# Seven-product projections: order of the combined activation blocks, banks of two kinds for transposes, and weight block sums emitted one step earlier

## The chip, the cores and the metric

The kernel runs on one core of a Trainium2 chip. A core has a matmul engine (TensorE, "PE" in the profile), a vector engine (VectorE, "DVE"), a scalar engine (ScalarE, "ACT"), GpSimd ("POOL") and SyncE ("SP", which here mostly starts DMAs). Each of them runs its own instructions strictly in the order written, and they meet at semaphores. The metric is the device time of one execution in microseconds; the number that counts is the median over runs of the same kernel.

## The reference

Two layers over a sequence of 1024 tokens of width 1024, all in fp32. Layer 0 has a gated delta network as its mixer, layer 1 a retention mixer; each is followed by a residual layer norm and a convolutional feed-forward block with hidden width 2816:

```python
for i in range(DEPTH):
    mod = (e @ ada_w[i] + ada_b[i])[:, None, :]
    sh1, sc1, g1, sh2, sc2, g2 = jnp.split(mod, 6, axis=-1)
    y = mixers[i % N_MIXERS](x * (1.0 + sc1) + sh1)
    x = layer_norm(DN_ALPHA * x + (1.0 + g1) * y, ln_g[i, 0], ln_b[i, 0])
    y = conv_ffn(x * (1.0 + sc2) + sh2, ffn_up[i], ffn_conv_w[i], ffn_conv_b[i], ffn_down[i])
    x = layer_norm(DN_ALPHA * x + (1.0 + g2) * y, ln_g[i, 1], ln_b[i, 1])

def conv_ffn(h, w_up, conv_w, conv_b, w_down):
    gate, up = jnp.split(h @ w_up, 2, axis=-1)
    gate = causal_dwconv(gate, conv_w) + conv_b
    return (jax.nn.silu(gate) * up) @ w_down
```

What the change touches are the large products of this: `h @ w_up` of both feed-forward blocks, the query, key and gate projections of the retention, and the three products that come back to width 1024 (`@ w_down` twice, the retention's `@ w_out` once).

## The kernel before, in words

**Precision.** Every fp32 operand of a product is split into a high part (ACT copies it to the fp32r type) and a low part (DVE subtracts the high part): the helper `split`, lines 89 and 90. A product is then three matmuls, low by high, high by low and high by high: lines 110 to 112 in the helper `mm3`. Line 90 on DVE is therefore the last step before PE can use any operand, and rows such as `wb L90` or `T L90` are named by the tile that was split.

**Seven products instead of eight.** A product of two 2 by 2 block matrices is done with seven block products (the Winograd form of Strassen's scheme). Two generators do this. `strassen` serves the projections whose activations stay in SBUF. Its activations are the blocks 11, 21, 12, 22 and four combinations: T1 = 12 - 11, T2 = 22 - T1, T3 = T2 - 11 (which is 22 - 12) and T4 = 21 - T2. Each block is four tiles, k = 0 to 3. `build_T` makes them, once for each of three projections (feed-forward 0 up at about 790 us, retention at about 1480 us, feed-forward 1 up at about 2345 us). I call these three places the borders. At a border the first two weight pairs (items 0 and 1) are multiplied plainly: `side(n, 0)` uses the blocks 11 and 21, `side(n, 1)` the blocks 12 and 22. `side(0, 0)` and `side(1, 0)` run while the rest of the activations are still being normalised; then `build_T` transposes the tiles of the lower half (four PE transposes into one PSUM bank, line 406; ACT scales and shifts the bank into a tile `bt`, line 408) and splits the blocks 12 and 22; then come `side(0, 1)`, the function `rest`, which makes T1 to T4, and `side(1, 1)`. From item 2 on, `wino` runs the seven products in the order 11, 21, T1, T2, 22, T3, T4. Its weights are combined by DVE into a PSUM bank (`psub`, line 1203: s1, s2, s4, s3) and split into a tile `wb`. The block 11 exists only as a high and a low part, so that adding it needs the sum of the two again: `joined` makes it with two matmuls by the identity into a PSUM bank (line 414).

**The way back.** `proj_gen` serves the three products that return to width 1024. The activation blocks, combined beforehand, are read from DRAM (tile `ar`, split to `ab`). The weight blocks are combined on the fly by `bblk` on DVE, for the products T1 (line 1302), T2 (line 1305, in place) and T4 (line 1308); the sum is split to `bb`. Each product has 11 steps (8 in the retention), and one step's work is emitted by `ops`. The weight blocks are loaded three steps ahead by `load_b`. When a product ends, its `f` function takes the four accumulators on DVE; `f2`, after the second product, makes the four tiles `c` (line 1383).

**Banks.** PSUM has eight banks of 128 by 512 floats: four with the tag `acc`, two with `mm`, two with `sc`. The transposes of `build_one` (line 259, for the blocks 11 and 21 while `proj_ln` or `proj_gen` still runs), those of `build_T` (line 406), `joined` and `psub` all draw from the two `mm` banks. The two `sc` banks serve every third product of `wino`, half of the accumulators in two of the products of `proj_gen`, and the squares of the layer norm.

**What sets the order.** The text of the kernel gives the dependencies. A scheduler then orders each engine's instructions once, by its own estimates of times, and the engines follow that order. So a change in the text shows only as far as it changes these orders.

## Time and profile before

| what | value |
|---|---|
| time, median of 3 runs | 3016.57 us (3015.99 to 3017.25) |
| profiled execution, its own time | 3017.08 us |
| its span, first to last instruction | 3015.3 us |
| granted TensorE clock, mean over the span | 0.975 |
| busy: PE, DVE, ACT, POOL | 94%, 73%, 45%, 21% |

A row of the timeline shows the start, the duration, the engine, the line of the kernel, the operation and its tiles; in brackets stands how long the engine was idle before it and what ended that idle time. A row of the groups shows the busy time, the mean duration, and after the bar the idle time ahead of the group. A row of the windows shows a stretch, its length, the busy time (and number of instructions) of PE, of its weight loads (PEld), of DVE, ACT and POOL, then the granted clock, the DMA share and the GB/s.

### The profile page before, as it was taken

Reading aid. Unit: us, or ns where it says so; the run is one execution under the profiler, and the core shown is the slowest. Engines: PE = TensorE matmul, PEld = TensorE weight load, DVE = VectorE, ACT = ScalarE, POOL = GpSimd, SP = SyncE. Lnnn points to the kernel's source line nnn. Section 1 sums busy time; section 2 is a strip of 40 time slices with the busy share of each in tenths; the row PEclk is TensorE's granted clock in tenths of the full one; section 3 lists DMA queues with packets and bytes.
Section 4 is the critical chain, followed back from the end, with each engine's and each line's share of the span. In section 5 each row is a group of like instructions: output and inputs, shape, how many; then the busy total and the mean of one; then the engine's idle time right before and its main releaser. Section 6 shows DMA issues by size and latency. Waiting matters only on the chain.

```text
span 3015.3 us, 38927 instructions
## 1 busy us (share of the span) xinstructions
PE 2843.1 (94%) x13638; PEld 2313.8 (77%) x13638; DVE 2196.9 (73%) x3845; ACT 1349.4 (45%) x2513; POOL 637.6 (21%) x629
## 2 busy tenths in 40 slices
PE   8889998999989999999999999989999899999997
PEld 7768877887768878777777787767777688888785
DVE  5795687545578888997688745556688787778888
ACT  4655555434544444536533343222336544445444
POOL 0411221133011111520023302522201011113503
PEclk9999999999999999999999999999999999999998
DMA  7222221343344444863423444656563333335652
GB/s 271 84 74 71 95 92 64 115 158 136 109 140 159 156 153 148 308 205 126 154 84 112 171 157 136 209 168 189 190 234 118 115 133 105 105 105 211 229 174 106
DMA packets 238708, 442.36 MB, mean 147 GB/s; under 512 B 22448, under 2 KB 75952, under 8 KB 238512
## 3 DMA queue, kind: packets, MB, share of 16 engines
q1 hardware_dynamic: 207328, 392.16, 38.6%
q10 hardware_dynamic: 29760, 43.00, 3.9%
q0 software_dynamic: 1424, 4.72, 0.4%
q8 instruction: 107, 1.75, 0.2%
q14 instruction: 89, 0.73, 0.1%
HBM read 331.26 MB, written 108.53 MB: 146 GB/s over the span
## 4 chain that ended last, share of the span: by engine, by line
PE 58%; DVE 16%; DMA 10%; issue 8%; ACT 4%; POOL 2%; SPq 1%; POOLq 0%; DVEq 0%; ACTq 0%
PE acc L635 14%; PE acc L1418 8%; PE acc L1157 6%; PE acc L110 4%; PE acc L111 4%; PE acc L112 4%; PE sc L1157 3%; PE sc L635 3%; PE mm L635 2%; PE sc L1418 2%; DVE ab L90 1%; PE sc L111 1%; PE sc L110 1%; PE sc L112 1%; DVE wb L90 1%
## 5 line engine op out<-in xcount | busy, mean ns | idle before, releaser
L1418 PE MATMUL acc<-bb,ab 128*128 128x512 f32 x1800 | 432.5, 393 | 7.7 <-DVE bb L90 5.8
L1418 PEld LDWEIGHTS acc<-bb,ab 128*128 128x128 f32 x1800 | 337.0, 189 | 85.0 <-DVE bb L90 10.3
L635 PE MATMUL acc<-hT,wh 128*128 128x512 f32 x960 | 302.6, 397 | 0.0
L1556 POOL TENSOR_TENSOR o<-o 128x512 f32<-128x512 f32 x88 | 119.0, 1363 | 723.8 <-DVE o L1549 716.1
L1157 PE MATMUL acc<-T,wb 128*128 128x512 f32 x840 | 209.6, 400 | 15.1 <-DVE wb L90 15.1
L635 PEld LDWEIGHTS acc<-hT,wh 128*128 128x128 f32 x960 | 184.2, 192 | 34.6
L635 PE MATMUL acc<-hT,wl 128*128 128x512 f32 x480 | 204.4, 426 | 0.2 <-ACT sg L1083 0.2
L1157 PEld LDWEIGHTS acc<-T,wb 128*128 128x128 f32 x840 | 160.6, 192 | 54.0 <-DVE wb L90 20.3
L90 DVE TENSOR_TENSOR ab<-ar,ab 128x512 fp32r<-128x512 f32 x210 | 179.4, 862 | 29.4 <-ACT ab L89 29.3
L89 ACT ACTIVATE ab<-ar 128x512 fp32r<-128x512 f32 x210 | 128.4, 623 | 134.3 <-PE acc L1418 73.3
L90 DVE TENSOR_TENSOR wb<-wr,wb 128x512 fp32r<-128x512 f32 x162 | 114.8, 711 | 100.1 <-ACT wb L89 97.3
L90 DVE TENSOR_TENSOR wl<-wr,wh 128x1024 fp32r<-128x1024 f32 x85 | 107.4, 1264 | 89.2 <-ACT wh L89 89.2
L89 ACT ACTIVATE wh<-wr 128x1024 fp32r<-128x1024 f32 x101 | 106.8, 1058 | 122.0 <-PE acc L635 55.7
L1214 ACT ACTIVATE pc<-acc 128x512 f32<-128x512 f32 x143 | 84.8, 593 | 169.5 <-PE acc L1157 98.6
L90 DVE TENSOR_TENSOR wb<-mm,wb 128x512 fp32r<-128x512 f32 x216 | 145.0, 684 | 21.2 <-ACT wb L89 19.2
L89 ACT ACTIVATE wb<-mm 128x512 fp32r<-128x512 f32 x216 | 122.5, 594 | 66.4 <-DVE mm L1203 66.3
L89 ACT ACTIVATE wb<-wr 128x512 fp32r<-128x512 f32 x162 | 98.8, 626 | 97.6 <-DMA wr<-in_ffn_up 51.3
L635 PE MATMUL acc<-wh,hT 128*128 128x512 f32 x384 | 137.1, 420 | 2.0 <-DVE vv L90 2.0
L1535 DVE SCALAR_TENSOR_TENSOR o<-g,vc,o 128x512 f32<-128x512 f32 (+2 forms) x176 | 135.8, 790 | 1.3 <-ACT o L1530 0.7
L454 DVE SCALAR_TENSOR_TENSOR qkv<-raw,vc,qkv 128x512 f32<-128x512 f32 x144 | 114.6, 800 | 25.9 <-ACT qkv L452 24.8
L89 ACT ACTIVATE bb<-Br 128x512 fp32r<-128x512 f32 x120 | 74.0, 624 | 123.1 <-DVE Br L1302 61.8
L110 PE MATMUL acc<-T,wb 128*128 128x512 f32 x292 | 116.3, 398 | 9.9 <-DVE wb L90 9.4
(618 smaller groups left out, 7148.3 us busy)
## 6 DMA issues: line engine op xcount, KB each, us to landing
wr<-in_ffn_up SPq DMA_DIRECT2D x96, 512.0 KB, 4.2
mvw<-in_ada_w SPq DMA_DIRECT2D x80, 512.0 KB, 4.4
ad<-o SPq DMA_DIRECT2D x154, 256.0 KB, 2.3
ar<-ad SPq DMA_DIRECT2D x154, 256.0 KB, 3.7
Br<-in_ffn_down SPq DMA_DIRECT2D x66, 256.0 KB, 3.9
wr<-in_ret_wv SPq DMA_DIRECT2D x32, 512.0 KB, 3.7
ar<-od SPq DMA_DIRECT2D x56, 256.0 KB, 4.4
xs<-xt ACTq DMA_DIRECT2D x24, 512.0 KB, 3.0
```

Of the source, the lines that this page charges most:

```text
L89: act.activation(dst_h, src, AF.Copy)
L90: eng.tensor_tensor(dst_l, src, dst_h, ALU.subtract)
L110: mm(acc, wl[:, k], hl[0], start=first, stop=False)
L111: mm(acc, wh[:, k], hl[1], start=False, stop=False)
L112: mm(acc, wh[:, k], hl[0], start=False, stop=last)
L454: dve.scalar_tensor_tensor(oh, raw[:, 3 - j:515 - j], w[:, 3 - j:4 - j], oh, ALU.mult, ALU.add)
L635: pq(pe.matmul(out, lhsT, rhs, start=start, stop=stop, **kw), cost)
L1157: return pe.matmul(*a, skip_group_check=True, **kw)
L1214: act.activation(t, X, AF.Copy)
L1418: mm_ = (lambda *a, p=p, onto=onto, **kw: (mm if p < 2 else pe.matmul)(*a, skip_group_check=onto, **kw))
L1535: dve.scalar_tensor_tensor(tv, gv[:, c0 - j:c1 - j], w[:, 2 - j:3 - j], tv, ALU.mult, ALU.add)
L1556: pool.tensor_tensor(o[d], o[x], o[y], op)
```

## The change

Three things are edited.

1. A counter `turn_tile` hands out `mm` and `sc` banks by turns. `build_one`, the loads of `build_T` and `joined` take their bank from it, so that they have four banks between them instead of two. `psub` stays on `mm`.
2. `rest` goes over the four tiles four times instead of once: all T1 (12 - 11), all T2 (22 - T1), all T3 (T2 - 11) and all T4 (21 - T2). T3 was 22 - 12 and needs the block 11 now, which is therefore joined twice: twelve pairs of joining matmuls at each border instead of eight. The numbers of subtractions (16) and of splits (16) stay. The tiles of T2 are now made in the place where `b22` was, and T1 and T3 in that of `b12`.
3. `proj_gen` makes the sum of the next step's weight block behind the present step's splits (`sum_ahead`), but not across the end of a product, other than behind the products 21, 22 and T3. The weight blocks are loaded four steps ahead.

```diff
@@ -63,6 +63,12 @@
 
     def sc_tile():
         return ps.tile([P, HALF], F32, tag="sc", name="sc", bufs=2)
+
+    nturn = [0]
+
+    def turn_tile():
+        nturn[0] += 1
+        return (mm_tile, sc_tile)[nturn[0] % 2]()
 
     def acc4():
         return [acc_tile(), acc_tile(), acc_tile(), acc_tile()]
@@ -254,7 +260,7 @@
         return scale, shift
 
     def build_one(tag, xts, scale, shift, f, eng=dve):
-        pt = mm_tile()
+        pt = turn_tile()
         for t in range(4):
             pe.transpose(pt[:, t * P:(t + 1) * P], xts[t][:, f * P:(f + 1) * P], ident)
         tmp = tl("t2", [P, HALF])
@@ -401,7 +407,7 @@
             B[nm][k] = t
 
         def load(f, tag):
-            pt = mm_tile()
+            pt = turn_tile()
             for t in range(4):
                 pe.transpose(pt[:, t * P:(t + 1) * P], xts[t][:, f * P:(f + 1) * P], ident)
             tmp = tl(tag, [P, HALF], name="bt")
@@ -409,7 +415,7 @@
             return tmp
 
         def joined(hl):
-            pt = mm_tile()
+            pt = turn_tile()
             for n, t in enumerate(hl):
                 pe.matmul(pt, ident_r, t, start=n == 0, stop=n == 1)
             return pt
@@ -422,17 +428,18 @@
             raw.append((b12, b22))
 
         def rest():
-            for k in range(4):
-                t1, b22 = raw[k]
-                x11 = joined(B["11"][k])
+            for k, (t1, b22) in enumerate(raw):
+                dve.tensor_sub(t1, t1, joined(B["11"][k]))
+                put("T1", k, t1)
+            for k, (t1, b22) in enumerate(raw):
                 dve.tensor_sub(b22, b22, t1)
-                put("T3", k, b22, pool if BAL["b3"] & 1 << k else dve)
-                dve.tensor_add(b22, b22, x11)
-                put("T2", k, b22, pool if BAL["bT"] & 1 << k else dve)
-                dve.tensor_sub(t1, t1, x11)
-                put("T1", k, t1, pool if BAL["b1"] & 1 << k else dve)
+                put("T2", k, b22)
+            for k, (t1, b22) in enumerate(raw):
+                dve.tensor_sub(t1, b22, joined(B["11"][k]))
+                put("T3", k, t1)
+            for k, (t1, b22) in enumerate(raw):
                 dve.tensor_sub(b22, joined(B["21"][k]), b22)
-                put("T4", k, b22, pool if BAL["b4"] & 1 << k else dve)
+                put("T4", k, b22)
 
         return rest
 
@@ -1309,11 +1316,17 @@
             return R[bn, j]
 
         nst = [0]
+        summed = {}
+
+        def sum_ahead(n):
+            if n < len(steps) and steps[n] not in summed:
+                summed[steps[n]] = bblk(*steps[n])
 
         def ops(an, bn, j, early):
-            ra, rb = ablk(an, j), bblk(bn, j)
             n = nst[0]
             nst[0] += 1
+            sum_ahead(n)
+            ra, rb = ablk(an, j), summed.pop((bn, j))
             last = an == "22"
             at = ltags[0] if last and j >= nj - ltags[3] else ("wl", "hTb", "wr")[n % 3] if early else ("wl", "wr")[n % 2]
             wt = ltags[1] if last and j >= nj - ltags[2] else ("wh", "hTb", "hTb")[n % 3] if early else "wh"
@@ -1323,6 +1336,8 @@
             split(w[0], w[1], rb)
             if bn == "22":
                 dve.tensor_tensor(X[j], rb, X[j], ALU.subtract)
+            if j < nj - 1 or bn in ("21", "22", "T3"):
+                sum_ahead(n + 1)
             return a, w
 
         xts = [[], []]
@@ -1409,7 +1424,7 @@
         prods = [("11", "11", f1), ("12", "21", f2), ("S1", "T1", f5), ("S4", "22", f3), ("S2", "T2", f6),
                  ("S3", "T3", f7), ("22", "T4", f4)]
         steps = [(bn, j) for _, bn, _ in prods for j in range(nj)]
-        ahead = 3
+        ahead = 4
         for st in steps[:ahead]:
             load_b(*st)
         hooks = []
```

The changed kernel's line numbers are 6 higher from the first edit on, 7 behind `build_T` and 15 behind `ops`. Of 9037 rows in PE's order 506 differ, of DVE's 3619 rows 502. The first difference on PE stands where the blocks 11 and 21 for feed-forward 0 are built.

**ACT, blocks 11 and 21 of feed-forward 0** (`t2` are the scaled transposes, `hT` the high parts, `wh_6760` the high part of a weight tile of the running projection). Before:

```order
L261 ACTIVATE t2_6517<-mm_6512,fh01_6112,fs01_6111 128x512
L261 ACTIVATE t2_6527<-mm_6522,fh01_6112,fs01_6111 128x512
L89 ACTIVATE hT_6519<-t2_6517 128x512
L89 ACTIVATE hT_6529<-t2_6527 128x512
L89 ACTIVATE wh_6760<-wr_6758 128x1024
L261 ACTIVATE t2_6573<-mm_6568,fh01_6112,fs01_6111 128x512
L261 ACTIVATE t2_6583<-mm_6578,fh01_6112,fs01_6111 128x512
L89 ACTIVATE hT_6575<-t2_6573 128x512
L261 ACTIVATE t2_6605<-mm_6600,fh01_6112,fs01_6111 128x512
L89 ACTIVATE hT_6585<-t2_6583 128x512
L89 ACTIVATE hT_6607<-t2_6605 128x512
```

Now:

```order
L267 ACTIVATE t2_6517<-sc_6512,fh01_6112,fs01_6111 128x512
L267 ACTIVATE t2_6527<-mm_6522,fh01_6112,fs01_6111 128x512
L267 ACTIVATE t2_6573<-sc_6568,fh01_6112,fs01_6111 128x512
L95 ACTIVATE hT_6519<-t2_6517 128x512
L95 ACTIVATE hT_6529<-t2_6527 128x512
L95 ACTIVATE hT_6575<-t2_6573 128x512
L267 ACTIVATE t2_6583<-mm_6578,fh01_6112,fs01_6111 128x512
L95 ACTIVATE hT_6585<-t2_6583 128x512
L95 ACTIVATE wh_6760<-wr_6758 128x1024
L267 ACTIVATE t2_6605<-sc_6600,fh01_6112,fs01_6111 128x512
L267 ACTIVATE t2_6615<-mm_6610,fh01_6112,fs01_6111 128x512
L267 ACTIVATE t2_6637<-sc_6632,fh01_6112,fs01_6111 128x512
```

Four builds instead of two stand ahead of the weight tile `wh_6760`, and four instead of six behind it.

**DVE and PE, the retention's border.** `T3`, `T1`, `T2`, `T4` are low parts of combined blocks, `bt` their sources, `mm_13212` (now `mm_13236`) is the weight combination s1, `wb_13233` (now `wb_13257`) its low part, with which the product T1 begins, and `pc` a partial result that takes in the product 21 from its bank. DVE before:

```order
L430 TENSOR_TENSOR bt_12950<-bt_12950,mm_13098 128x512
L432 TENSOR_TENSOR bt_12943<-bt_12943,mm_13098 128x512
L1203 TENSOR_TENSOR mm_13212<-wr_13191 128x512
L90 TENSOR_TENSOR T2_13107<-bt_12950,T2_13107 128x512
L90 TENSOR_TENSOR T1_13111<-bt_12943,T1_13111 128x512
L434 TENSOR_TENSOR bt_12950<-mm_13114,bt_12950 128x512
L1203 TENSOR_TENSOR mm_13231<-mm_13212,wr_13190 128x512
L90 TENSOR_TENSOR T4_13119<-bt_12950,T4_13118 128x512
L90 TENSOR_TENSOR wb_13233<-mm_13212,wb_13233 128x512
L1203 TENSOR_TENSOR mm_13251<-wr_13190,mm_13231 128x512
L1148 TENSOR_TENSOR pc_13210<-sc_13217,pc_13210 128x512
```

DVE now:

```order
L441 TENSOR_TENSOR bt_12902<-sc_13114,bt_12902 128x512
L441 TENSOR_TENSOR bt_12922<-mm_13122,bt_12922 128x512
L441 TENSOR_TENSOR bt_12942<-sc_13130,bt_12942 128x512
L441 TENSOR_TENSOR bt_12962<-mm_13138,bt_12962 128x512
L1210 TENSOR_TENSOR mm_13236<-wr_13215 128x512
L96 TENSOR_TENSOR T4_13119<-bt_12902,T4_13118 128x512
L96 TENSOR_TENSOR T4_13127<-bt_12922,T4_13126 128x512
L96 TENSOR_TENSOR T4_13135<-bt_12942,T4_13134 128x512
L1210 TENSOR_TENSOR mm_13255<-mm_13236,wr_13214 128x512
L96 TENSOR_TENSOR T4_13143<-bt_12962,T4_13142 128x512
L1155 TENSOR_TENSOR pc_13234<-sc_13241,pc_13234 128x512
L96 TENSOR_TENSOR wb_13257<-mm_13236,wb_13257 128x512
```

The low part of s1 now stands behind the addition that reads the product 21 (line 1155, before 1148), which it stood ahead of. Between it and the low part of the weights for the products 11 and 21 (`wb_13194`, now `wb_13218`) there were 13 rows, and now there are 23. On PE, four joins stand now between the products 11 and 21 (`sc_13241` is the bank of the product 21):

```order
L118 MATMUL acc_13221<-hT_12245,wb_13218 128x512
L420 MATMUL sc_13114<-hT_12255,ident_r_727 128x512 x2
L420 MATMUL mm_13122<-hT_12265,ident_r_727 128x512 x2
L420 MATMUL sc_13130<-hT_12295,ident_r_727 128x512 x2
L420 MATMUL mm_13138<-hT_12305,ident_r_727 128x512 x2
L116 MATMUL sc_13241<-hT_12255,wb_13238 128x512
L117 MATMUL sc_13241<-hT_12255,wb_13238 128x512
```

Before, three single joins stood spread over `side(1, 1)` instead; the last of them is the first row here, and the product 11 follows:

```order
L414 MATMUL mm_13114<-hT_12293,ident_r_727 128x512 x2
L112 MATMUL acc_13159<-22_12955,wh_13155 128x512
L110 MATMUL acc_13197<-hT_12183,wb_13194 128x512
```

The joins that stood in `side(1, 1)` are collected behind the product 11.

**DVE, start of the product T1 in the way back of feed-forward 0** (`c` are the four results of the product before, `Br` sums of weight blocks, `ab` and `bb` the low parts with which the product T1 begins). Before:

```order
L90 TENSOR_TENSOR bb_11200<-Br_11149,bb_11200 128x512
L1383 TENSOR_TENSOR c_11211<-acc_10701,rowb_7702 128x512
L1383 TENSOR_TENSOR c_11219<-acc_10702,rowb_7702 128x512
L1383 TENSOR_TENSOR c_11227<-acc_10703,rowb_7702 128x512
L1383 TENSOR_TENSOR c_11235<-acc_10704,rowb_7702 128x512
L1302 TENSOR_TENSOR Br_11243<-Bw_11171,Bw_10696 128x512
L1302 TENSOR_TENSOR Br_11274<-Bw_11193,Bw_10696 128x512
L1302 TENSOR_TENSOR Br_11298<-Bw_11203,Bw_10699 128x512
L90 TENSOR_TENSOR ab_11245<-ar_11241,ab_11245 128x512
```

Now:

```order
L96 TENSOR_TENSOR bb_11214<-Br_11136,bb_11214 128x512
L1398 TENSOR_TENSOR c_11227<-acc_10714,rowb_7714 128x512
L1398 TENSOR_TENSOR c_11235<-acc_10715,rowb_7714 128x512
L1398 TENSOR_TENSOR c_11243<-acc_10716,rowb_7714 128x512
L1398 TENSOR_TENSOR c_11251<-acc_10717,rowb_7714 128x512
L1309 TENSOR_TENSOR Br_11265<-Bw_11185,Bw_10708 128x512
L1309 TENSOR_TENSOR Br_11296<-Bw_11207,Bw_10711 128x512
L1309 TENSOR_TENSOR Br_11320<-Bw_11219,Bw_10711 128x512
L96 TENSOR_TENSOR ab_11259<-ar_11257,ab_11259 128x512
L96 TENSOR_TENSOR bb_11262<-Br_11217,bb_11262 128x512
```

The first sum, `Br_11217`, was made twelve rows ahead of this piece; three other sums have come up behind the `c`, so that `ab` is as far from the last `c` as it was.

## The prediction

> **What bounds the kernel now.** I read the page first, then the waits of PE, then the timeline of PE, DVE and ACT at the edited places.
>
> ```profile
> PE 2843.1 (94%) x13638; PEld 2313.8 (77%) x13638; DVE 2196.9 (73%) x3845; ACT 1349.4 (45%) x2513; POOL 637.6 (21%) x629
> L259 PE MATMUL mm<-cst,xt 128*128 128x128 f32 x96 | 15.2, 275 | 3.9 <-ACT t L261 3.2 <-ACT xt L297 0.7
> L406 PE MATMUL mm<-cst,xt 128*128 128x128 f32 x96 | 15.1, 289 | 2.9 <-ACT bt L408 2.8
> L414 PE MATMUL mm<-hT,ident_r 128*128 128x512 f32 x48 | 14.9, 409 | 1.2 <-DVE bt L434 0.6 <-ACT bt L408 0.6
> PE acc L1418 <- DVE bb L90: 5.8, 7, 1.5
> ```
>
> PE is busy 94% of the span, so what counts is PE's own work and its gaps of about 172 us. The three groups of transposes and joins show that PE waits only 3.9 + 2.9 + 1.2 = 8.0 us for their banks and tiles in the whole program: that is all that more banks can return directly. The gaps at the borders are larger, and another engine sets them:
>
> ```profile
> 834.92 0.79 PE L110 MATMUL acc<-T,wb 128*128 128x512 f32 x1 [4.69 <-DVE wb L90]
> 842.22 4.53 PE L1157 MATMUL acc<-T,wb 128*128 128x512 f32 x12 [1.96 <-DVE wb L90]
> 2389.06 0.50 PE L110 MATMUL acc<-T,wb 128*128 128x512 f32 x1 [4.69 <-DVE wb L90]
> 2396.36 3.91 PE L1157 MATMUL acc<-T,wb 128*128 128x512 f32 x9 [2.68 <-DVE wb L90]
> 830.87 3.39 DVE L1535 SCALAR_TENSOR_TENSOR o<-g,vc,o 128x512 f32<-128x512 f32 x5
> 834.18 0.68 DVE L90 TENSOR_TENSOR wb<-mm,wb 128x512 fp32r<-128x512 f32 x1
> ```
>
> The product T1 of both feed-forward borders waits 4.69 us for the split *weights* of s1, which stand on DVE behind the convolutions of line 1535, and not for the block T1. DVE in its order is the bound there. A gap also costs clock:
>
> ```profile
> 742.00:747.00 5.00, 5.00 (x12) 3.92 (x13) 4.19 (x10) 0.00 (x0) 0.00 (x0) 0.50 0.80 311
> 747.00:752.00 5.00, 5.00 (x22) 4.05 (x21) 0.70 (x2) 0.00 (x0) 0.00 (x0) 0.92 0.15 46
> ```
>
> Behind a gap of 2.46 us (741.79, below) five microseconds hold 12 matmuls at clock 0.50, then 22: some 2.3 us are lost on top of the gap.
>
> **The change part by part.** The sum is made against the profiled execution, 3017.08 us (0.5 above the median of 3016.57).
>
> *Builds for feed-forward 0: -2.1.*
>
> ```profile
> 733.34 1.06 ACT L89 ACTIVATE wh<-wr 128x1024 fp32r<-128x1024 f32 x1 [2.23 <-PE acc L317]
> 734.30 1.43 ACT L261 ACTIVATE t<-mm,fh,fs 128x512 f32<-128x512 f32 x2
> 741.03 0.63 ACT L89 ACTIVATE hT<-t 128x512 fp32r<-128x512 f32 x1
> 738.68 0.66 PE L259 MATMUL mm<-cst,xt 128*128 128x128 f32 x4 [1.05 <-ACT t L261]
> 741.79 0.79 PE L315 MATMUL acc<-wh,hl 128*128 128x512 f32 x1 [2.46 <-DVE t L345]
> ```
>
> ACT stands idle 2.23 us at the weight tile, then works through six builds from 734.30 to 741.66, 1.23 us each, and PE's next product starts at 741.79. With four builds ahead of the weight tile, two of the six leave: -2.45. They take about 2 x 1.23 = 2.45 in an idle time of 2.23, so the tile may start up to 0.4 later: -2.1. The bounds are 0 (the tile is late by as much) and -7.3 (all the builds' gaps, 5.0 with the smaller ones before them, and the 2.3 of slow clock). I take the value near the ACT rows. The last gap, to line 345, remains, so the clock does too.
>
> *Other transposes: -0.5.* ```profile
> 791.82 1.79 PE L406 MATMUL mm<-cst,xt 128*128 128x128 f32 x8 [2.08 <-ACT bt L408]
> 2349.29 0.66 PE L406 MATMUL mm<-cst,xt 128*128 128x128 f32 x4 [0.73 <-ACT bt L408]
> 2356.27 1.20 PE L414 MATMUL mm<-hT,ident_r 128*128 128x512 f32 x4 [0.58 <-ACT bt L408]
> ```
>
> 8.0 less the 2.6 of the builds up to 738.68 leaves 5.4. Of that 2.1 stand at feed-forward 0's border (791.82), where ACT's pace and not the bank sets the time; the two gaps of feed-forward 1's border, 0.73 and 0.58, are counted there. Bounds 0 and -3.
>
> *Extra joins.* 24 matmuls more; one after another they start 0.23 us apart (below, 1515.95 and 1516.18), so a border has 4 x 2 x 0.23 = 1.8 us more PE work, 5.5 in all. Before the second half of `side` four joins more stand inside `side(0, 1)`, at every border.
>
> *Feed-forward borders: +1.4 and +0.6.*
>
> ```profile
> 812.61 0.50 PE L110 MATMUL acc<-12_7055,wl 128*128 128x512 f32 x1 [1.00 <-DVE wl L90]
> 818.60 1.29 DVE L90 TENSOR_TENSOR wb<-wr,wb 128x512 fp32r<-128x512 f32 x2 [2.03 <-ACT wb L89]
> 822.40 1.30 DVE L90 TENSOR_TENSOR T<-bt,T 128x512 fp32r<-128x512 f32 x2 [0.70 <-ACT T L89]
> ```
>
> The weights for the products 11 and 21 (818.60) wait for PE to finish the first half of `side(1, 1)`, which starts when `side(0, 1)` has ended: 1.8 later. Behind them DVE has 24 rows up to s1's low part, before 23: +0.6. Idle times of 1.2 behind 818.60 can be used up. So the product T1, bound by DVE, starts 1.8 + 0.6 - 1.0 = 1.4 later. At feed-forward 1 the banks can take away up to 1.3 us of gaps (0.73 and 0.58 above), and 0.6 is left. Bounds for each: -1.3 and +2.4. Should DVE not set this end, the 4.69 us cover the joins entirely.
>
> *The retention's border: +5.*
>
> ```profile
> 1500.73 0.50 PE L110 MATMUL acc<-12_12892,wl 128*128 128x512 f32 x1 [1.25 <-DVE wl L90]
> 1506.06 0.63 ACT L89 ACTIVATE wb<-wr 128x512 fp32r<-128x512 f32 x1 [0.18 <-PE acc L110]
> 1507.93 0.68 DVE L90 TENSOR_TENSOR wb<-wr,wb 128x512 fp32r<-128x512 f32 x1
> 1508.53 3.09 DVE L90 TENSOR_TENSOR T<-bt,T 128x512 fp32r<-128x512 f32 x5
> 1515.95 0.39 PE L110 MATMUL sc<-hT,wb 128*128 128x512 f32 x1
> 1516.18 0.39 PE L111 MATMUL sc<-hT,wb 128*128 128x512 f32 x1
> 1517.91 0.68 DVE L90 TENSOR_TENSOR wb<-mm,wb 128x512 fp32r<-128x512 f32 x1
> 1518.67 0.47 PE L110 MATMUL acc<-T,wb 128*128 128x512 f32 x1
> ```
>
> Here T1 starts without a gap (1518.67, 2.72 after the product 21). Now the four joins in `side(0, 1)` bring PE +1.8; three single joins leave `side(1, 1)`, -1.4; four stand ahead of the product 21, +1.8: it starts 2.2 later, at 1518.2, and ends at 1520.9. DVE's second `wb` comes at 1507.93 + 1.8 = 1509.7. From there to the end of s1's low part are 24 rows at 0.61 us (3.09 / 5, the five splits at 1508.53), so that ends at about 1524.4; before, the 14 rows from 1507.93 on took 9.98. It cannot end before about 1522.4 anyway, since the addition that reads the finished product 21 stands ahead of it. T1 then starts between 1522.4 and 1524.4, 3.7 to 5.7 later, with a new gap of 1.5 to 3.5 us, which may cost up to 2.3 of clock. What is queued behind it on DVE is s2 and s4, for which T2 and 22 wait; DVE has idle times later, PE has none that gives the shift back. I take +5; bounds +1.5 (the splits moved ahead fill DVE's idle times, no gap) and +8.
>
> The Trainium skill, page "TensorE: Matmul & The Clock Gate", section "What's actually happening", says that the clock halves after an idle window of about 3.4 us. By this rule the new gap would mostly cost no clock, and this term would be nearer +4. The trace differs: the gaps of 1.96 (842.22: 12 matmuls in 4.53 us) and 2.46 us are followed by the slow rate.
>
> *Weight block sums ahead: -1.5.*
>
> ```profile
> 1294.46 0.69 DVE L1383 TENSOR_TENSOR c<-acc,rowb 128x512 f32<-128x512 f32 x1 [0.67 <-PE acc L1418]
> 1295.07 1.89 DVE L1302 TENSOR_TENSOR Br<-Bw 128x512 f32<-128x512 f32 x3
> 1296.87 0.69 DVE L90 TENSOR_TENSOR ab<-ar,ab 128x512 fp32r<-128x512 f32 x1
> 1297.70 1.19 PE L1418 MATMUL sc<-bb,ab 128*128 128x512 f32 x2 [3.28 <-ACT bb L89]
> 2203.80 1.69 PE L1418 MATMUL sc<-bb,ab 128*128 128x512 f32 x6 [3.45 <-DVE ab L90]
> 2838.02 1.19 PE L1418 MATMUL sc<-bb,ab 128*128 128x512 f32 x2 [3.28 <-ACT bb L89]
> 1276.59 6.00 DVE L90 TENSOR_TENSOR ab<-ar,ab 128x512 fp32r<-128x512 f32 x1
> 1276.98 5.04 POOL L1346 TENSOR_TENSOR xt<-xt,rowb 128x512 f32<-128x512 f32 x4
> ```
>
> At the start of T1 PE's 3.28 us end with `ab` on DVE (1296.87 + 0.69 = 1297.56; the row names ACT), which stands behind the last `c` and three sums of 0.63 us. In the new order one sum is gone from there and another has come up: the three waits (10.0 us) stay. A gain can come in the other waits of accumulators for `bb`, 5.8 us in seven: a sum of about 0.7 leaves the chain ahead of three or four of them, here -1.5 in all. Had the sum been hidden, 0. The other bound is +3: the first sum moves to about 1283, where DVE's rows run beside POOL and one takes 6.00 us; the four results `c` behind it have idle times ahead of them, 0.67 us the last, that take in a part.
>
> The Trainium skill, page "SBUF — State Buffer", section "Practical consequences", says of this that a VectorE instruction with two SBUF inputs contends with a GpSimd instruction that reads SBUF, and the loser blocks. The 6.00 us row agrees; by the rule alone this term would be up to +3 at feed-forward 0 and 0 elsewhere.
>
> Sum: -2.1 - 0.5 + 1.4 + 0.6 + 5 - 1.5 = +2.9, so 3020.0 for an execution like the profiled one, and 3019.5 for the median.
>
> **The rivals.**
>
> *The gaps go.* With T1 complete earlier the feed-forward borders lose their 4.69 us each and 2.3 of clock behind each: -14.0. With the -4.1 of the other gains and +5 at the retention: 3016.57 - 13.1, 3003.5. For it speaks that T1 is complete on DVE 20 rows earlier than before. Against it: the gaps end with `wb`, and as many rows as before stand ahead of it.
>
> *The pushed splits decide everywhere.* Where DVE's rows between the two `wb` need longer than PE's work (at the retention from 1509.7 to the end of the product 21 at 1520.9, 11.2 us, or 18 rows of 0.61), each row more is paid by PE in full. There 24 rows are 14.6 us: beyond the point. If this holds with the upper bounds, +8 + 2.4 + 2.4, and the builds and sums bring nothing against the -4.1: 3016.6 + 12.8 = 3029.4; with half of those gains 3027.3. Against it: DVE has idle times of 2.7 us in the same stretch of feed-forward 0 (2.03 and 0.70) that it can use.
>
> *Nothing is seen.* The 5.5 us of joins lie in the gaps that DVE leaves, the gaps stay, and the retention's DVE catches up: 3016.6. Against it: no gap covers the four joins ahead of the retention's product 21.
>
> **How the numbers follow.** Forecast 0.42 (3019.5, its own range 3014 to 3024), gaps go 0.22, pushed splits 0.22, nothing seen 0.14. A measurement here cannot tell less than 0.2%, 6.0 us, from no change. Faster than 3010.5 are nearly all of the second and a little of the first: 0.24. Slower than 3022.6 are the third and a fifth of the forecast: 0.30. The rest, 0.46, is the same. The range 3006 to 3028 leaves out the lower half of the gaps that go, and the end of the pushed splits.
>
> **What would show it.** Right: a new gap of 1.5 to 3.5 us ahead of the retention's product T1, which ends with `wb`; the gaps of 4.69 and of about 3.3 us still there; ACT's idle time ahead of the weight tile near 731 gone and PE's start behind it about 2 earlier; 72 joins of 0.23 us. Wrong: the 4.69 us shrink by more than 2, or the retention's T1 starts without a gap, or PE waits for `sc` banks.

## The result and the profile after

| | before | after |
|---|---|---|
| median of 15 runs each | 3016.57 us (3005.97 to 3023.51) | 3023.00 us (3015.69 to 3031.89) |
| profiled execution | 3017.08 us | 3026.40 us |
| its span | 3015.3 us | 3024.6 us |
| mean granted clock | 0.975 | 0.977 |

The ratio is 1.0026, with a 95% interval of 1.0014 to 1.0037: the change makes the kernel slower by about 8 us at this ratio (6.4 us by the medians). That is a little beyond the 0.2% that such a measurement can tell from nothing. The predicted 3019.5 us is 3.5 us too fast; the measured time lies in the range, and in the forecast's own narrower one. "The same" had the highest chance, 0.46; "slower", which it is by a narrow margin, had 0.30.

The page of the kernel after and its groups and waits, beside what the prediction showed of before (lines moved by 6 to 15: 90 is now 96, 110 to 112 are 116 to 118, 1157 is 1164, 1418 is 1433):

```profile
PE 2840.7 (94%) x13662; PEld 2316.9 (77%) x13662; DVE 2188.5 (72%) x3845; ACT 1350.2 (45%) x2513; POOL 627.3 (21%) x629
L265 PE MATMUL sc<-cst,xt 128*128 128x128 f32 x48 | 9.8, 285 | 0.5 <-ACT xt L303 0.5
L412 PE MATMUL sc<-cst,xt 128*128 128x128 f32 x48 | 8.3, 275 | 1.9 <-ACT bt L414 1.9
L420 PE MATMUL sc<-hT,ident_r 128*128 128x512 f32 x36 | 11.3, 399 | 0.0
L420 PE MATMUL mm<-hT,ident_r 128*128 128x512 f32 x36 | 11.2, 400 | 1.0 <-DVE bt L438 1.0
PE acc L1433 <- DVE bb L96: 11.9, 11, 1.9
L1315 DVE TENSOR_TENSOR Br<-Br,Bw 128x512 f32<-128x512 f32 x30 | 20.7, 689 | 14.9 <-DMA Br<-in_ffn_down 10.5 <-DMA Br<-in_ret_wout 4.3
```

The groups of transposes and joins together now wait 0.5 + 1.9 + 1.0 = 3.4 us instead of 8.0 (the two groups of transposes on `mm` banks, left out here, show 0.0), so the banks do what they were meant to do. On the other side PE waits 11.9 us instead of 5.8 us for `bb`. The last row is DVE's sum for the product T4; the same group of the kernel before is this:

```profile
L1308 DVE TENSOR_TENSOR Br<-Br,Bw 128x512 f32<-128x512 f32 x30 | 20.7, 692 | 4.6 <-DMA Br<-in_ffn_down 3.1 <-DMA Br<-in_ret_wout 1.1
```

DVE stands idle ahead of these thirty sums for 14.9 us instead of 4.6, and what ends the idle time is the load of the weight block. PE's timeline of after at the edited places:

```profile
711.13 0.50 PE L321 MATMUL acc<-wh,hl 128*128 128x512 f32 x1 [0.75 <-DVE t L351]
738.48 0.79 PE L321 MATMUL acc<-wh,hl 128*128 128x512 f32 x1 [4.50 <-DVE t L351]
830.64 0.79 PE L116 MATMUL acc<-T,wb 128*128 128x512 f32 x1 [4.31 <-DVE wb L96]
837.94 2.35 PE L1164 MATMUL acc<-T,wb 128*128 128x512 f32 x6 [2.16 <-DVE wb L96]
1295.32 0.70 PE L1433 MATMUL sc<-bb,ab 128*128 128x512 f32 x2 [3.28 <-ACT ab L95]
1504.14 0.73 PE L116 MATMUL acc<-12_12904,wl 128*128 128x512 f32 x1 [1.97 <-DVE wl L96]
1527.91 0.62 PE L116 MATMUL acc<-T,wb 128*128 128x512 f32 x1 [3.58 <-DVE wb L96]
2398.44 0.73 PE L116 MATMUL acc<-T,wb 128*128 128x512 f32 x1 [4.31 <-DVE wb L96]
2405.74 4.42 PE L1164 MATMUL acc<-T,wb 128*128 128x512 f32 x12 [2.69 <-DVE wb L96]
```

The gaps ahead of the product T1 at both feed-forward borders are still there (4.31, before 4.69). The retention's T1, which had none, now has one of 3.58 us, and it ends with `wb`. The gap at the builds became one of 4.50 us where there had been four of together 5.0.

Where the time went is told best by stretches between two matmuls that stand at the same place of the work in every kernel. In before the marks are these rows and the rows of T1 in the prediction; the other kernels have the same ones:

```profile
712.84 0.50 PE L315 MATMUL acc<-wh,hl 128*128 128x512 f32 x1 [0.75 <-DVE t L345]
1231.61 3.60 PE L1418 MATMUL acc<-bb,ab 128*128 128x512 f32 x15
1448.58 11.04 PE L635 MATMUL acc<-bb,ab 128*128 128x512 f32 x48
```

- Builds: from the matmul at 712.84 (after: 711.13) to the one behind the last gap of the builds (741.79, after 738.48): 28.95 us before, 27.35 after.
- Builds and border of feed-forward 0: from the same matmul to the first T1 matmul (834.92, after 830.64): 122.08, 119.51.
- Way back 0: from the first matmul on `bb` and `ab` (1231.61) to the end of the last (1448.58 + 11.04 = 1459.62): 228.01, and 233.79 after.
- Retention's border: from there to its first T1 matmul (1518.67; after 1527.91): 59.05, 65.99.
- Border of feed-forward 1: the same for its own way back and T1: 64.85, 64.68.

In the profiled executions the stretches so have -1.7 ahead of the first edit, -2.6, +5.8, +6.9 and -0.2. The stretches between them are the large products, the other two ways back and the end. They sum to +1.1, which makes the +9.3 us between the two spans.

### The profile page after: what moved, and what is told of

The parts are those of the page before. It is cut to its first block, busy times and chain, and to the rows that moved or that the text cites. A ratio compares the mean times of both kernels' runs of the same rounds, so it can differ in the third digit from the quotient of the medians.

```text
span 3024.6 us, 38954 instructions
## 1 busy us (share of the span) xinstructions
PE 2840.7 (94%) x13662; PEld 2316.9 (77%) x13662; DVE 2188.5 (72%) x3845; ACT 1350.2 (45%) x2513; POOL 627.3 (21%) x629
## 5 line engine op out<-in xcount | busy, mean ns | idle before, releaser
L1433 PE MATMUL acc<-bb,ab 128*128 128x512 f32 x1800 | 432.9, 394 | 16.8 <-DVE bb L96 11.9
L1164 PE MATMUL acc<-T,wb 128*128 128x512 f32 x840 | 207.9, 397 | 15.0 <-DVE wb L96 14.9
L96 DVE TENSOR_TENSOR ab<-ar,ab 128x512 fp32r<-128x512 f32 x210 | 172.0, 824 | 23.9 <-ACT ab L95 23.7
L222 DVE SCALAR_TENSOR_TENSOR ada<-mvw,e,ada 128x512 f32<-128x512 f32 x140 | 108.0, 772 | 28.4 <-DMA mvw<-in_ada_w 28.2
```

Of the source, the lines that this page charges most:

```text
L96: eng.tensor_tensor(dst_l, src, dst_h, ALU.subtract)
L222: dve.scalar_tensor_tensor(a, wr[:, kk], e[:, k:k + 1], a, ALU.mult, ALU.add)
L1164: return pe.matmul(*a, skip_group_check=True, **kw)
L1433: mm_ = (lambda *a, p=p, onto=onto, **kw: (mm if p < 2 else pe.matmul)(*a, skip_group_check=onto, **kw))
```

## The experiments

The kernels of a group ran side by side with before, and only the ratios compare between groups, since before had a median of 3007.70 in the first, 3009.57 in the second and 3007.95 in the third. Each median is of twelve runs, that of the order of `rest` alone of six. All stretches are from one profiled execution of each kernel, and all diffs are against the kernel after:

| kernel | time, us | ratio to before (95%) | builds | builds and border 0 | way back 0 | retention's border | border 1 |
|---|---|---|---|---|---|---|---|
| before | | | 28.95 | 122.08 | 228.01 | 59.05 | 64.85 |
| after | 3023.00 | 1.0026 (1.0014 to 1.0037) | 27.35 | 119.51 | 233.79 | 65.99 | 64.68 |
| banks alone | 3007.17 | 1.0002 (0.9987 to 1.0016) | 27.36 | 120.81 | 228.24 | 59.01 | 64.96 |
| order of `rest` alone | 3019.71 | 1.0043 (1.0028 to 1.0057) | 28.93 | 125.39 | 227.06 | 66.89 | 70.21 |
| sums and loads alone | 3011.03 | 1.0010 (0.9998 to 1.0023) | 29.24 | 122.44 | 233.89 | 59.07 | 65.17 |
| old order at the retention | 3011.81 | 1.0010 (0.9998 to 1.0022) | 27.38 | 118.92 | 234.81 | 59.00 | 64.67 |
| the same, no sums ahead | 3006.19 | 0.9990 (0.9973 to 1.0006) | 27.36 | 119.45 | 228.95 | 59.01 | 64.68 |
| the same, sums of T1 and T2 ahead | 3006.09 | 0.9982 (0.9968 to 0.9995) | 27.37 | 119.99 | 227.41 | 58.98 | 64.68 |
| retention's T4 late | 3016.69 | 1.0014 (0.9998 to 1.0029) | 27.38 | 119.00 | 239.32 | 61.84 | 64.68 |
| joins alone on four banks | 3007.26 | 0.9988 (0.9975 to 1.0000) | 28.97 | 119.61 | 228.53 | 64.17 | 64.53 |
| after without sums ahead | 3011.31 | 0.9997 (0.9981 to 1.0013) | 27.35 | 119.97 | 227.94 | 64.42 | 64.67 |
| after, T4's sum in its own step | 3016.05 | 1.0018 (1.0001 to 1.0034) | 27.37 | 118.93 | 236.88 | 64.38 | 64.67 |
| after once more | 3016.64 | 1.0019 (1.0001 to 1.0037) | 27.37 | 119.49 | 237.48 | 66.01 | 64.66 |
| after, loads six ahead | 3021.36 | 1.0040 (1.0027 to 1.0054) | 27.39 | 119.41 | 235.23 | 64.41 | 64.66 |

Where the code of a stretch is the same, the builds and border 1 repeat to about 0.3 us. Builds and border 0 together differ by up to 1.1 us (118.92 to 119.99 in the nine kernels that have all four banks and the new order there), the retention's border by 1.6 (64.4 or 66.0 with the new order; the last section shows why), and way back 0 by up to 2 us, or 6 with loads four ahead. So a stretch tells a part from another where the times, with intervals of about 4 us to each side, cannot. The long stretches between them tell nothing: from the retention's T1 to the next way back, the same kernel after needs 607.68 us in one execution and 597.25 in the other.

### First: the three parts, each alone

The banks alone: `turn_tile` stays, the other two parts are undone.

```diff
-            for k, (t1, b22) in enumerate(raw):
-                dve.tensor_sub(t1, t1, joined(B["11"][k]))
-                put("T1", k, t1)
...
+            for k in range(4):
+                t1, b22 = raw[k]
+                x11 = joined(B["11"][k])
...
-        ahead = 4
+        ahead = 3
```

> The banks alone: transposes and joins take mm and sc banks by turns, everything else as before (rest over k once, sums not ahead, loads three steps ahead). My theory: the four builds of feed-forward 0 stand ahead of the weight tile as in the changed kernel, PE starts behind them 1.6 to 2.1 us earlier, and at feed-forward 1's border the two gaps of 0.73 and 0.58 us go: 2 to 4 us faster than before, no new gap at the retention's border. Rival (the shared sc banks make PE wait): slower by 2 to 4 us, with waits of PE for an sc bank in the rows.

The builds gain 1.6 us (28.95 to 27.36). At the product T1 1.3 of it is left, which is hardly more than this stretch differs by itself. No other stretch moves by more than 0.3 us; the gain expected at feed-forward 1's border does not arrive. There PE waits longer instead: the gaps ahead of T1 grow from 4.69 us to 5.91 at feed-forward 0 and 5.35 at feed-forward 1, so what PE gains ahead of T1 it waits for DVE. The ratio of 1.0002 sees nothing of that, as it must with an interval of 4 us to each side.

The new order of `rest` alone, on two banks:

```diff
-        pt = turn_tile()
+        pt = mm_tile()
```

(at all three places, and `ahead = 3` without `sum_ahead`)

> The order of the combined blocks alone: rest goes over the tiles four times with twelve joins, all on the two mm banks, sums as before. My theory: the retention's border holds the loss. In this kernel's DVE order the addition that reads the product 21 stands ahead of all T4 rows, so s1's low part comes even later than in the changed kernel: the product T1 starts 5 to 9 us later there; the feed-forward borders within 1.5 us either way: 4 to 9 us slower than before. Rival (what costs are the 24 added matmuls): 5.5 us slower, spread evenly over the three borders at 1.8 us each.

It has the highest ratio of all: 1.0043, 12 us by the medians. Every border grows: 3.3, 7.8 and 5.4 us; the expectation had left the feed-forward borders within 1.5 us. The timelines of DVE and PE at feed-forward 0's border in this run:

```profile
804.15 1.29 DVE L432 TENSOR_TENSOR bt<-bt,mm 128x512 f32<-128x512 f32 x2 [3.01 <-PE mm L420]
826.86 1.38 DVE L441 TENSOR_TENSOR bt<-mm,bt 128x512 f32<-128x512 f32 x2 [3.16 <-PE mm L420]
836.92 0.80 PE L116 MATMUL acc<-T,wb 128*128 128x512 f32 x1 [8.26 <-DVE wb L96]
```

DVE waits 3.01 and 3.16 us for joins that PE has not yet made, and the gap ahead of T1 becomes 8.26 us, where it was 4.69. With two banks, of which `psub` takes its share, PE cannot run ahead with the joins of four tiles. The new order therefore needs the banks; alone it is a loss.

The sums and the loads alone:

```diff
-        pt = turn_tile()
+        pt = mm_tile()
...
-            for k, (t1, b22) in enumerate(raw):
-                dve.tensor_sub(t1, t1, joined(B["11"][k]))
-                put("T1", k, t1)
...
+            for k in range(4):
+                t1, b22 = raw[k]
+                x11 = joined(B["11"][k])
```

(that is, after with the banks and `rest` of before; `sum_ahead` and four steps of loading stay)

> The weight block sums one step ahead alone, with loads four steps ahead. Theory by the trace of the changed kernel: the sum for T4 (in place on the loaded block) waits for its load at the head of DVE's order, 14.9 us of idle time on DVE instead of 4.6, and PE's waits for bb grow by 4 to 6 us near 1390 to 1440: 3 to 6 us slower than before. Rival (the prediction's term): the sums leave the chain ahead of bb, 1.5 us faster.

The borders stay as they were, and way back 0 grows by 5.9 us. So the loss in that stretch comes with the third part (with the other two alone it is 228.24 and 227.06). The ratio of 1.0010 has 1 just inside its interval.

### The retention's border

After, with the old order of `rest` at the retention alone:

```diff
-        return rest
+        return rest_old if old else rest_new
...
-        rest = build_T(B, xts, scale, shift, tags)
+        rest = build_T(B, xts, scale, shift, tags, direct)
```

> The changed kernel, with the former order of rest (one pass over the tiles, eight joins) at the retention's border alone. My theory: the new gap of 3.6 us ahead of the retention's product T1 is gone and that border is 5 to 6 us shorter than in the changed kernel: 3017 to 3018, within 2 us of before. Rival (the loss sits elsewhere, and the gap is covered later by PE's other waits in the retention): 3021 to 3023.

The border is back at 59.00 us, from 65.99, and the ratio falls from 1.0026 to 1.0010. The border of feed-forward 0 keeps what it had gained. What happens with the new order is to be read in DVE's timeline of after, between its two splits named `wb`:

```profile
1512.75 0.69 DVE L96 TENSOR_TENSOR wb<-wr,wb 128x512 fp32r<-128x512 f32 x1 [0.31 <-ACT wb L95]
1513.36 1.29 DVE L96 TENSOR_TENSOR T<-bt,T 128x512 fp32r<-128x512 f32 x2
1514.57 0.68 DVE L438 TENSOR_TENSOR bt<-bt,sc 128x512 f32<-128x512 f32 x1
...
1522.37 0.69 DVE L441 TENSOR_TENSOR bt<-mm,bt 128x512 f32<-128x512 f32 x1
1522.96 0.69 DVE L1210 TENSOR_TENSOR mm<-wr 128x512 f32<-128x512 f32 x1
1523.57 1.89 DVE L96 TENSOR_TENSOR T<-bt,T 128x512 fp32r<-128x512 f32 x3
...
1526.57 0.69 DVE L1155 TENSOR_TENSOR pc<-sc,pc 128x512 f32<-128x512 f32 x1
1527.17 0.68 DVE L96 TENSOR_TENSOR wb<-mm,wb 128x512 fp32r<-128x512 f32 x1
```

From 1512.75 to 1527.85 there is no idle time: 25 rows in 15.1 us, 0.60 each. PE has finished the product 21 at 1524.33 (its last matmul starts at 1523.94 and takes 0.39) and stands still to 1527.91. The splits of T2, T3 and T4, of which nothing is needed for the product T1, stand ahead of the weights of the first. And the clock falls behind the gap:

```profile
1523.00:1528.00 5.00, 1.42 (x7) 0.84 (x5) 4.96 (x10) 1.31 (x3) 0.00 (x0) 1.00 0.00 0
1528.00:1533.00 5.00, 5.00 (x15) 3.96 (x16) 3.17 (x5) 2.13 (x4) 0.00 (x0) 0.66 0.15 16
```

These are windows of after. The 5 us behind the gap hold 15 matmuls at clock 0.66; in the kernel before the five from 1518.60 on hold 24 at clock 1.00:

```profile
1518.60:1523.60 5.00, 5.00 (x24) 4.13 (x23) 3.95 (x7) 2.69 (x5) 0.00 (x0) 1.00 0.10 21
```

Nine matmuls less at 0.23 us are about 2 us. Counted from the first matmul on a block 12, T1 comes 6.1 us later than before (35.24 to 41.32) and the product 22 7.7 us (40.77 to 48.49).

If the gap comes from the rows that stand ahead of `wb`, taking away the four joins and eight DVE rows of T4 should remove it. In this kernel the retention's T4 is made behind the product T1:

```diff
+        def late():
             for k, (t1, b22) in enumerate(raw):
                 dve.tensor_sub(b22, joined(B["21"][k]), b22)
                 put("T4", k, b22)
```

> The changed kernel, with T4 at the retention's border made behind the product T1 instead of ahead of it; joins, banks and sums stay. Between the weights of the products 11 and 21 and the low part of s1 DVE has 15 rows then instead of 23. My theory (the pushed rows make the gap): T1 starts 4 to 5 us earlier than in the changed kernel, its gap of 3.6 shrinks below 2; a part comes back as a gap of 1 to 3 us ahead of T2: 2 to 4 us faster than the changed kernel. Rival (the twelve joins and their place cost it): as the changed kernel.

PE's timeline of that run:

```profile
1523.37 0.50 PE L116 MATMUL acc<-T,wb 128*128 128x512 f32 x1
1527.67 0.72 PE L420 MATMUL mm<-hT,ident_r 128*128 128x512 f32 x2 [0.78 <-DVE bt L443]
1532.23 5.49 PE L1166 MATMUL acc<-T,wb 128*128 128x512 f32 x12 [3.83 <-DVE wb L96]
```

The gap ahead of T1 is gone and that border is 4.2 us shorter (65.99 to 61.84). But one of 3.83 us stands ahead of T2 now, with its slow clock (12 matmuls in 5.49 us), and the product 22 starts 51.32 us behind the first matmul on a block 12, later than in after (48.49). The ratio of 1.0014 cannot be told from that of after (1.0026, and 1.0019 once more), where 2 to 4 us less had been expected. DVE's work of the border is the bound; a row moved past one product stands ahead of the next. The cause of the gap is confirmed by this and the remedy is not one.

### What the feed-forward borders gain, and from which banks

Joins on four banks, transposes on two, no sums:

```diff
         def load(f, tag):
-            pt = turn_tile()
+            pt = mm_tile()
```

(and the same in `build_one`; `joined` keeps `turn_tile`, and there is no `sum_ahead`, with `ahead = 3`)

> The new order of rest at all borders with the joins alone on banks of two kinds; transposes on the two mm banks, sums as before. It tells which user needs the four banks. If the joins do (in the order alone on two banks DVE waits twice for 3 us for a join), the feed-forward borders come to 39.6 to 40.5 us, as in the changed kernel, and the retention's to 41 to 43: 4 to 6 us slower than before in all. If the transposes do, the feed-forward borders stay near 46 us: 10 to 13 slower.

It is the joins that need the four banks. Counted from the first matmul on a block 12 to T1, the two feed-forward borders take 39.44 and 40.27 us here, 39.59 and 40.04 in after, and 46.18 and 46.54 with the new order on two banks.

The builds are back at 28.97 us, as their transposes have only two banks. But the whole stretch to T1 is 119.61, the same as in after. So two gains that look as if they add up do not. After comes 1.6 us earlier to the transposes of the border (77.40 us behind the first mark, here 78.99), and needs as much longer from there to T1 (42.11 us, here 40.62; before 43.10). What makes it longer was not isolated. The retention's border stays long (64.17). The loss of 4 to 6 us that the expectation had did not come: the ratio is 0.9988.

### The sums and the loads

With the old order at the retention and loads three ahead, first without sums ahead:

```diff
-            sum_ahead(n)
-            ra, rb = ablk(an, j), summed.pop((bn, j))
...
+            ra, rb = ablk(an, j), bblk(bn, j)
...
-        ahead = 4
+        ahead = 3
```

> Banks of two kinds everywhere, the new order of rest at the two feed-forward borders, the former order at the retention's, weight block sums and loads as before. If the parts add up as the borders' lengths in the earlier profiles say (builds -1.6, feed-forward borders -2.1 and -1.4, retention's border -0.9, sums left out): about 6 us, 0.2%, faster than before. Rival (the profiles' gains are given back later, as the banks alone did not show more than 0.02%): within 2 us of before.

and then with the sums of the products T1 and T2 ahead, T4's in its own step:

```diff
-            if j < nj - 1 or bn in ("21", "22", "T3"):
+            if bn not in ("T3", "T4") and (j < nj - 1 or bn in ("21", "22")):
                 sum_ahead(n + 1)
...
-        ahead = 4
+        ahead = 3
```

> The same, with the sums one step ahead for T1 and T2 alone; the sum for T4, which works in place on a block loaded just before, stays in its own step, and loads stay three steps ahead. My theory (the wait on the load at the head of DVE's order is what the sums cost): DVE's idle time at the T4 sum falls from 14 to about 5 us, PE's waits for bb in accumulators fall from 10 to about 6, and the time is that of the mix without sums, within 1 us. Rival (having sums early costs by itself, beside POOL or by its place in the order): 2 to 4 us slower than the mix without sums.

Without sums ahead the ratio is 0.9990 and way back 0 is at 228.95 us; with the sums of T1 and T2 ahead it is 0.9982 and 227.41. The second is the only kernel whose interval lies wholly below 1: 3006.09 against 3009.57 us. That is 0.18%, and the only one of thirteen ratios, so I take it for a hint of a gain over before and no more; from after's ratio, 1.0026 or 1.0019, its interval is apart. The difference between the two, 0.0008 or 2.4 us, is inside the intervals.

From this I took it that the early sum of T4 is what costs, since it was the one thing left out. Three kernels of the third group asked that. After with no sums ahead, and loads three ahead (the first of the two diffs above, without the old order at the retention):

> The changed kernel without its third part: banks of two kinds and the new order of rest everywhere, sums and loads as before. My theory (the sums cost 3 to 6 us, by DVE's wait on the load of the T4 block): 3 to 6 us faster than the changed kernel beside it, DVE's idle time at the T4 sum near 4. Rival (the sums cost nothing, the third part's waits of PE are covered): as the changed kernel.

After with T4's sum in its own step, and loads four ahead as in after:

```diff
-            if j < nj - 1 or bn in ("21", "22", "T3"):
+            if bn not in ("T3", "T4") and (j < nj - 1 or bn in ("21", "22")):
                 sum_ahead(n + 1)
```

> The changed kernel with the T4 sum back in its own step; T1 and T2 sums one step ahead, loads four steps ahead. If the T4 sum alone is the cost, this is as fast as the kernel without any sums ahead, within 2 us, with DVE's idle time at that sum near 5 instead of 14.9. If the early T1 and T2 sums or the earlier loads cost too, it stays in between.

And after, unchanged, as the measure for both:

> The changed kernel once more, on the chip of the three others of this set. Expected as measured: 0.14 to 0.37% slower than before, 4 to 11 us; border lengths, from the first product of the block 12 to the start of T1, of 39.6, 41.3 and 40.0 us.

My theory falls. With T4's sum in its own step the ratio is 1.0018, with it ahead 1.0019; with no sums ahead and loads three ahead it is 0.9997. DVE's order around T4 has the same pattern of sums and splits in the two. What separates the kernels is how many steps ahead the blocks are loaded. For seven kernels, DVE's idle time ahead of T4's sum and PE's wait for `bb`:

| kernel | sums ahead | loads ahead | idle ahead of T4's sum | PE waits for `bb` | way back 0 |
|---|---|---|---|---|---|
| before | none | 3 | 4.6 | 5.8 | 228.01 |
| after without sums | none | 3 | 2.8 | 3.5 | 227.94 |
| sums of T1 and T2 | T1, T2 | 3 | 5.3 | 3.2 | 227.41 |
| T4's sum in its step | T1, T2 | 4 | 15.1 | 14.2 | 236.88 |
| after once more | T1, T2, T4 | 4 | 17.0 | 13.6 | 237.48 |
| sums and loads alone | T1, T2, T4 | 4 | 13.3 | 10.3 | 233.89 |
| loads six ahead | T1, T2, T4 | 6 | 9.1 | 5.4 | 235.23 |

The idle times are the groups' rows, of which these are the two that matter, of the kernel with T1 and T2 at depth 3 and of the one with T4's sum in its step at depth 4:

```profile
L1328 DVE TENSOR_TENSOR Br<-Br,Bw 128x512 f32<-128x512 f32 x30 | 20.7, 690 | 5.3 <-DMA Br<-in_ret_wout 3.1 <-DMA Br<-in_ffn_down 2.0
L1315 DVE TENSOR_TENSOR Br<-Br,Bw 128x512 f32<-128x512 f32 x30 | 20.7, 689 | 15.1 <-DMA Br<-in_ffn_down 10.3 <-DMA Br<-in_ret_wout 4.7
```

These two kernels have the same sums ahead, and differ in the depth and in the retention's border, which comes after way back 0. That stretch has 227.41 in the one and 236.88 in the other; the retention's order alone moves it by 1.0 us in the two other pairs (228.95 and 227.95; 234.81 and 233.79). Over all kernels it is 227.1 to 229.0 in the seven with loads three ahead and 233.8 to 239.3 in the six with four, with no overlap. The timelines of after, of SP, DVE and PE, show the cost at T4:

```profile
1380.75 0.33 SPq L1300 DMA_DIRECT2D Br<-in_ffn_down  x1
1383.62 0.69 DVE L1315 TENSOR_TENSOR Br<-Br,Bw 128x512 f32<-128x512 f32 x1 [2.30 <-DMA Br<-in_ffn_down]
1400.95 0.69 DVE L1315 TENSOR_TENSOR Br<-Br,Bw 128x512 f32<-128x512 f32 x1 [1.45 <-DMA Br<-in_ffn_down]
1408.98 0.69 DVE L1315 TENSOR_TENSOR Br<-Br,Bw 128x512 f32<-128x512 f32 x1 [0.85 <-DMA Br<-in_ffn_down]
1392.46 8.87 PE L1433 MATMUL acc<-bb,ab 128*128 128x512 f32 x36 [1.34 <-DVE bb L96]
1402.43 3.06 PE L1433 MATMUL acc<-bb,ab 128*128 128x512 f32 x12 [1.11 <-DVE bb L96]
1411.06 2.93 PE L1433 MATMUL acc<-bb,ab 128*128 128x512 f32 x8 [1.92 <-DVE bb L96]
```

The loads do go out a little earlier: this one at 1380.75, in before at 1385.60, which is 152.6 and 154.0 us behind the first matmul of the stretch. But the sum that needs it has moved up by as much (1383.62; before 1388.83: 155.5 and 157.2 us), it is reached before the block has landed, and everything behind it on DVE, the splits of `bb` for which PE waits among it, stands still. In the same part of this product PE had three waits in before, of 0.31, 0.37 and 0.33 us. That the scheduler moved the sums up because its estimate had the earlier loads landed is my reading of the orders. It was not separated by a run: loads four ahead with no sums ahead was not tried.

Is more depth the cure?

```diff
-        ahead = 4
+        ahead = 6
```

> The changed kernel with the weight blocks loaded six steps ahead instead of four. If the T4 sum waits since its load is issued too late, DVE's idle time there falls from 14.9 to below 6 and the kernel gains 3 to 6 us on the changed one. Rival (loads are held by their buffers or by what stands ahead of them on SyncE, not by the step they are written in): idle time and total as in the changed kernel, or slower, since activation blocks come later.

The idle time shrinks (9.1), less than expected, and nothing is gained: 1.0040, beside 1.0019 for after, with intervals that overlap. In the last way back, which takes 226.8 us from its first matmul to its last (before 222.4, after 219.4), PE now waits for `ab`, the activations' split:

```profile
2855.87 2.23 PE L1433 MATMUL sc<-bb,ab 128*128 128x512 f32 x6 [3.82 <-DVE ab L96]
2984.88 13.24 PE L642 MATMUL acc<-bb,ab 128*128 128x512 f32 x57 [2.68 <-DVE ab L96]
```

So the depth moves the wait from one operand to the other. Three steps are the best of the three depths tried.

The number in the text does not set how far ahead a load runs, and in this the rival of the expectation is borne out. From the issue of a block's load to the start of its sum, the eleven steps of T4 in way back 0 have 2.61 to 4.77 us in before (three steps), 2.65 to 4.89 in after (four) and 2.59 to 4.84 with six. SyncE stands still ahead of these loads until splits on DVE have ended: between 1345 and 1420 us for 17.8 us on `ab` in before, and in after for 11.0 us on `bb` and 6.4 on `ab`. The text lets these tiles share one set of 24 buffers, so the loads seem to wait for a buffer; that reading was not tested by a run. What a larger number changes is the order, and with it where DVE meets a block that has not landed.

## Why the prediction was right in part

**Retention's border, +5: right.** The gap of 1.5 to 3.5 us that ends with `wb` came, with 3.58. The rows between the two `wb` are there, at 0.60 us; from the one to the end of the other they are 25, where the prediction counted 24. The stretch grew by 6.9, of which 1.6 is a half clock inside the second half of `side`, behind the gap of 1.97 at 1504.14. That was not foreseen, and three other kernels with the same code and the same gap don't have it (64.38 to 64.42, about +5.3), while after once more does (66.01). In one of the three, after without sums, the parts of the term can be read: counted from the end of way back 0, the second `wb` starts 49.26 us later, before 48.31, so 1.0 later and not 1.8; and from there to T1 it is 15.15 us, before 10.74, so 4.4 more and not 3.9. That the two errors cancel is luck. The times of the two pairs that differ in this border alone (1.0010 to 1.0019 or 1.0026; 0.9990 to 0.9997) say 2 to 5 us, within their intervals.

**Builds, -2.1, and other transposes, -0.5: right, a little large.** 1.6 us in each of the ten kernels that have the edit (27.35 to 27.39), and ACT's idle time of 2.23 us ahead of the weight tile is gone. Whether any of it reaches T1 depends on the other edits.

**Feed-forward borders, +1.4 and +0.6: the sign is wrong.** The builds and the border together have -2.6, where my terms came to about -1.2 for them; feed-forward 1's border has -0.2. The step that failed is that `side(0, 1)` would end 1.8 us later for its four joins more. From the transposes behind the gap of 2.08 us in the prediction's row at 791.82 (1.86 us in after, row below) to the end of `side(0, 1)` PE needs 17.53 us instead of 17.65.

```profile
788.53 0.66 PE L412 MATMUL sc<-cst,xt 128*128 128x128 f32 x4 [1.86 <-ACT bt L414]
```

The four banks of the transposes are not the reason, since with the joins alone on four banks the gap is still 2.08 us and the same way takes 17.11. The clock may be a part of it. In the 5 us behind that gap it was 0.66 in before and in the sums and loads alone, the two kernels with the old order on two banks, and 1.00 in after and in the joins alone; a third of 5 us is 1.7 us, about as much as the four joins cost. But with the banks alone it was 1.00 too, and the way took 18.33. So the step is known that failed, and its cause stays open. The rest of the step held: DVE's idle times are used up (from 815.71 to the end of `wb` at 830.59 it has none), the gap remains, and it ends with `wb`.

**Weight block sums, -1.5: the step that failed worst.** I costed the sums and forgot the loads. I gave the fourth step of loading no price, though it changes SP's order and with it where DVE meets a block that has not landed. Measured were +5.8 in way back 0 (the five other kernels with loads four ahead: +5.9 to +11.3). In the last way back the matmuls end 2.6 us earlier on average of the six kernels, and the work behind the last matmul takes 1.8 longer. The three waits of about 3.3 us ahead of the products T1 stayed, as predicted; and the sums of T1 and T2 alone may bring the small gain that I had put down (0.9982 against 0.9990), though the intervals don't separate them.

**The rivals.** "The gaps go" fell: 4.31 remains of 4.69. "Nothing is seen" fell at the retention. "Pushed splits decide everywhere" is right at the retention and wrong at the feed-forward borders, where DVE had idle time to give; it would be right at all three on two banks (the order of `rest` alone, +3.3, +7.8 and +5.4).

The sum: -2.6, -0.2, +6.9 and +5.8 make +9.9 where the prediction had +2.9; with the -1.7 and +1.1 of the other stretches this is the profiled execution's +9.3. The terms at the borders were off by about -1.4, -0.8 and +1.9, which nearly cancel, and the loads by +7.3. That the measured median lies inside the forecast's own range is therefore partly luck: the loss of 5.8 us in way back 0 has a cause that the forecast did not have, and it did not carry the sum out of the range.

## What to carry to other kernels

Before moving work ahead on an engine that runs in order, ask what stands behind it: making all of one block first serves the first product only if the splits of the others do not then stand ahead of that product's other operand. A load issued earlier is no gain by itself where the consumer is moved up as far; look at the idle time ahead of the consumer, not at the issue. And time the parts apart: here the banks with the new order at two of the three borders cost nothing and may gain a little, and the order at the third border and the fourth step of loading took more than that. And the number of steps ahead in the text need not be the distance on the chip: measure the time from a load's issue to its use.

## What the runs showed of the hardware that was not expected

A gap of 1.97 us ahead of the same matmul, in the same code, was followed by a half clock in some executions and not in others. First after, then after without sums:

```profile
1504.00:1507.00 3.00, 2.86 (x7) 2.30 (x8) 1.31 (x2) 0.26 (x1) 0.00 (x0) 0.54 0.79 247
```

```profile
1497.00:1500.00 3.00, 2.84 (x12) 2.36 (x13) 1.33 (x2) 0.28 (x1) 0.00 (x0) 1.00 0.74 262
```

Seven matmuls in the 3 us at clock 0.54, or twelve at 1.00: the stretch from there to T1 takes 23.77 us in the two executions of after, and 22.14 in after without sums and in the two other kernels with this gap at full clock (T4's sum in its own step, loads six ahead). With the retention's T4 late the clock fell too (0.58 in those 3 us). So it fell in three executions of six. At feed-forward 0's border the gap of 2.08 us was followed by a clock of 0.66 over 5 us in two kernels and of 1.00 in two. The Trainium skill, page "TensorE: Matmul & The Clock Gate", section "What's actually happening", has the clock fall to half after at least one idle window of about 3.4 us, and has these windows run free. By this rule no gap shorter than a window costs clock; these runs show that one of 1.97 us can, and that it need not. The gap of 3.56 to 3.59 us ahead of the retention's T1 was followed by slow matmuls (0.63 us each) in all six executions that have it, in after from the first one on, in after without sums only from the sixth.
